# A convolution in two partial sums, one of them in PSUM, and new costs in the planner that orders the issue

## The chip, the core and the metric

The kernel runs on one core of a Trainium2 chip (trn2). The metric is the device time of one execution in microseconds; for the kernel before, three runs took 2491.57, 2493.82 and 2495.34 us, with a median of 2493.82.

## What is computed

One layer of a hybrid decoder, on 2048 prompt tokens with 16 meta tokens ahead of them and on 8 single tokens of running sequences. All data is float32.

```python
z = einsum('btd,dc->btc', rmsnorm(h, norm1_g), w_in)
q_r, f_r, i_r, g_r, a_r, b_r = split(z, IN_SPLITS)
o, s_new = hgrn2(q, k, v, logf, s0)                  # 4 heads of 128 x 128, in chunks of 64 tokens
y_hg = rmsnorm(o, hg_onorm_g) * silu(g_r)
glu = a_r * sigmoid(b_r)
xcat = concatenate([buf, glu], axis=1)
dw = depthwise_conv(xcat, conv_w) + conv_b           # 31 taps, 512 channels
y_cv = silu(layernorm(dw, conv_ln_g, conv_ln_b))
h = h + concatenate([y_hg, y_cv], axis=-1) @ w_out
h = h + square(relu(rmsnorm(h, norm2_g) @ w_up)) @ w_down
y = rmsnorm(h, final_g)
```

## The kernel before

**Phases.** The prompt is worked in four quarters of 512 tokens (`NQ`, `QT`). The mixing phase runs, for each quarter, 24 column pieces of `w_in` and 8 of `w_out`, in the order in(0), in(1), out(0), in(2), out(1), in(3), out(2), out(3). Each product of float32 is made of three passes with high and low parts, so a piece is 24 matmuls of 512 columns (in quarter 0, 48 of 260 or 268); these are the foreground matmuls. The MLP phase follows, in two halves of the tokens, with foreground matmuls nearly alone.

**Planner.** Nothing is left to a scheduler: the text emits every instruction in the order in which its engine takes it, and the order comes from an estimate that runs along in Python. `Model` keeps a time for each engine; `Proxy` gives each instruction a cost by its form and calls `Model.op`. Everything that isn't a foreground matmul is a generator in `Background`: it yields the name of the engine that it wants next, and `Background.ready` resumes it when the estimate says that its input is there and that the engine isn't too far ahead of TensorE. So the estimate never changes what is computed, only the place of each instruction in its engine's order. Where the foreground needs something that isn't done by the estimate, `Background.until` lets the estimate run on and emits background work, with no foreground matmul between, until it is.

**Heads.** `hgrn` is the chain of one head in one quarter: scan and reciprocal on VectorE (the tiles `B` and `I`), transposes of `I` on TensorE, score and state matmuls, then the head's output in a PSUM bank. That is normalised by four ScalarE squares with a sum (`junk,stat<-ps`), twelve VectorE instructions on 4 columns that make an inverse root (`rsqrt`, tiles `stat` and `kept`), four ScalarE scalings into `on`, which shares its buffer with `KPn`, and four TensorE transposes of it (`ps<-ident,KPn`). A head's tiles `F`, `K`, `Q`, `V` come from rings of two, so the head after next waits for it. The last product of a head is `ps<-Sch,Q`.

**Convolution.** `conv` works one quarter and one of four groups of 128 channels. Each of its 31 taps yields "any": if ScalarE and GpSimd have room by the estimate, ScalarE scales the shifted input by the tap's weight into a scratch buffer and GpSimd adds it (a side tap); otherwise VectorE does the tap in one instruction. All add into the same accumulator `acc_` in SBUF, one after the other:

```python
elif bg.choice == "dve" or len(scr.items) <= 3:
    V.scalar_tensor_tensor(out=acc_, in0=src, scalar=w, in1=acc_, op0=ALU.mult, op1=ALU.add)
else:
    t = scr.take()[0]
    S.activation(t, src, AF.Copy, scale=w)
    G.tensor_tensor(acc_, acc_, t, ALU.add)
```

`ln` normalises the four groups of a quarter when all are done; `out` of the quarter waits for it and for the heads. Background work has four PSUM banks. Scratch buffers of 512 columns: eleven, shared by accumulators, side taps and residuals.

In the views every instruction that the planner records has one line, L146 before and L167 after, so groups are told apart by their tiles: `scr<-glu,cw` is a tap.

Of the kernel before, what the change touches and what calls it, by code (L numbers as in the profile page):

```python
# [8 lines left out]
F32R = mybir.dt.float32r  # L9
# [68 lines left out]
class Model:  # L78
# [4 lines left out]
    def __init__(self):  # L83
        self.t = {"pe": 0.0, "dve": 0.0, "act": 0.0, "pool": 0.0, "dma": 0.0}
        self.cur = Ctx()
# [21 lines left out]
class Proxy:  # L107
# [3 lines left out]
    def __getattr__(self, f):  # L111
        fn, name, model = getattr(self._eng, f), self._name, self._model

        def call(*args, **kw):
# [6 lines left out]
            else:  # L121
                n = _size(out)
                if name == "pe":
                    rhs = kw.get("rhs")
                    if f == "transpose" or rhs.dtype != F32R:
                        cost = max(17 + 0.72 * n, 60.0) if f == "transpose" else max(1.67 * n, 214.0)
                        if n == 1:
                            cost = 425.0
                    else:
                        cost = 2.6 + 0.4167 * n  # L130
                elif name == "act":
                    cost = 130 + 0.8 * n
                    if not isinstance(kw.get("scale", 1.0), float):
                        cost += 100
                elif name == "pool":
                    cost = 60 + 2.2 * n
                elif f == "reciprocal":
                    cost = 60 + 6.3 * n
                elif f in ("bn_stats", "tensor_reduce"):
                    cost = 65 + 1.05 * _size(args[1])  # L140
                elif f in ("tensor_copy", "memset"):
                    cost = 65 + 0.53 * n
                else:
                    cost = 68 + 1.1 * n
                model.op(name, cost)
# [5 lines left out]
class Background:  # L151
# [13 lines left out]
    def ready(self, entry):  # L165
# [58 lines left out]
def tile_hybrid_step(  # L224
# [565 lines left out]
    with tc.manual_schedule():  # L790
# [3 lines left out]
        with ExitStack() as p1:  # L794
# [285 lines left out]
            dw = {}  # L1080
# [599 lines left out]
```

## Time and profile before

| | us |
|---|---|
| runs, median of 3 | 2493.82 |
| profiled execution, own time | 2496.16 |
| its span, first to last instruction | 2494.4 |
| PE busy, of the span | 2359.6 (95%) |
| DVE, ACT, POOL busy | 1192.5, 775.4, 750.4 |
| granted clock, mean share | 0.979 |

PE is TensorE, PEld its weight loads, DVE VectorE, ACT ScalarE, POOL GpSimd, SP SyncE, which issues the DMAs. A form is out<-in by the program's names, buffer numbers left out, with partitions x elements. The idle time in front of an instruction is given with what ended it. Busy time counts an instruction from start to end, so a VectorE instruction that is held up while it runs shows as a longer one, not as idle time.

### The profile page before, as it was taken

The numbers are of one execution on the slowest core, as the hardware profiler recorded it, in microseconds if no ns is written. First come the engines' busy times: TensorE is split into PE (matmuls) and PEld (weight loads), VectorE is DVE, ScalarE is ACT, GpSimd is POOL, SyncE is SP. The second block draws the span as 40 slices with busy tenths as digits, with TensorE's granted clock in tenths as the row PEclk, the third lists the DMA queues.
The fourth block names the chain that finished last, engine by engine and source line by source line (L and its number), as shares of the span: only waits on it lengthen the run. The fifth ranks groups of instructions, "written<-read, shape, count | busy, mean of one in ns | idle before, by whom it ended". The sixth has DMA issues, their size and how long they took to land.

```text
span 2494.4 us, 31897 instructions
## 1 busy us (share of the span) xinstructions
PE 2359.6 (95%) x13000; PEld 2101.0 (84%) x13000; DVE 1192.5 (48%) x1843; ACT 775.4 (31%) x1391; POOL 750.4 (30%) x476
## 2 busy tenths in 40 slices
PE   8877889899999699999999999999999999999998
PEld 8876777877777488999999999999888888888887
DVE  6798787657566964343233233225722122212225
ACT  6544566466546434312112112113201101100112
POOL 4565567667855721321222121221000000000000
PEclk9998999999999899999999999999999999999999
DMA  8664453853474257854444444447722222222222
GB/s 293 217 193 163 158 178 121 274 213 135 156 249 170 90 192 283 275 163 140 129 152 135 141 139 144 127 152 261 262 102 92 94 102 85 101 98 88 101 85 102
DMA packets 159224, 396.29 MB, mean 159 GB/s; under 512 B 8772, under 2 KB 107657, under 8 KB 125278
## 3 DMA queue, kind: packets, MB, share of 16 engines
q1 hardware_dynamic: 158934, 394.00, 46.4%
q8 instruction: 102, 1.67, 0.3%
q14 instruction: 44, 0.36, 0.0%
q10 hardware_dynamic: 144, 0.26, 0.0%
HBM read 265.91 MB, written 128.79 MB: 158 GB/s over the span
## 4 chain that ended last, share of the span: by engine, by line
PE 72%; DVE 17%; ACT 4%; DMA 3%; issue 2%; POOL 1%; SPq 0%; ACTq 0%; DVEq 0%; POOLq 0%
PE ps L146 72%; DVE scr L146 5%; DVE stat L146 3%; DVE kept L146 2%; ACT scr L146 2%; DVE I L146 1%; DMA raw<-in_w_in_dram 1%; DVE B L146 1%; DVE K L146 1%; DVE act L146 1%; DMA scr<-xscr 1%; POOL scr L146 1%; ACT act L146 1%; DVE glu L146 1%; DVE xn L146 1%
## 5 line engine op out<-in xcount | busy, mean ns | idle before, releaser
L146 PE MATMUL ps<-act,wsp 128*128 128x512 f32 (+5 forms) x7704 | 1504.7, 354 | 14.4 <-POOL wsp L146 8.1
L146 PEld LDWEIGHTS ps<-act,wsp 128*128 128x128 f32 x7704 | 1284.4, 191 | 176.6 <-POOL wsp L146 8.9
L146 PE MATMUL ps<-hid,wsp 128*128 128x344 f32 (+4 forms) x3864 | 713.4, 346 | 2.0 <-DMA wsp<-kw 1.9
L146 PEld LDWEIGHTS ps<-hid,wsp 128*128 128x128 f32 x3864 | 646.5, 188 | 64.8 <-DVE acc L146 1.5
L146 POOL TENSOR_TENSOR scr<-scr 128x512 f32<-128x512 f32 x330 | 466.6, 1434 | 265.2 <-ACT scr L146 202.3
L146 POOL TENSOR_TENSOR wsp<-raw,wsp 128x1024 fp32r<-128x1024 f32 (+1 forms) x98 | 237.5, 2424 | 589.6 <-ACT wsp L146 563.6
L146 DVE TENSOR_TENSOR acc<-ps,acc 128x1032 f32<-128x1032 f32 (+5 forms) x160 | 162.0, 1013 | 469.1 <-PE ps L146 469.0
L146 ACT ACTIVATE xn<-ps 128x1032 f32<-128x1032 f32 (+5 forms) x74 | 69.1, 934 | 838.1 <-PE ps L146 835.3
L146 DVE TENSOR_TENSOR xn<-xn 128x1032 f32<-128x1032 f32 (+3 forms) x68 | 80.3, 1181 | 508.0 <-ACT hid L146 508.0
L146 ACT ACTIVATE scr<-glu,cw 128x512 f32<-128x512 f32 x330 | 222.8, 716 | 19.2 <-POOL scr L146 15.8
L146 ACT ACTIVATE wsp<-raw 128x1024 fp32r<-128x1024 f32 (+1 forms) x98 | 101.5, 1036 | 302.9 <-PE ps L146 223.2
L146 DVE SCALAR_TENSOR_TENSOR scr<-glu,cw,scr 128x512 f32<-128x512 f32 x150 | 155.8, 1071 | 12.3 <-POOL scr L146 11.5
L146 DVE TENSOR_TENSOR hid<-xn,hid 128x1032 fp32r<-128x1032 f32 (+3 forms) x68 | 133.5, 1963 | 2.4
L146 ACT ACTIVATE junk<-ps 128x128 bf16<-128x128 f32 (+3 forms) x100 | 38.3, 383 | 109.7 <-PE ps L146 80.2
L146 ACT ACTIVATE hid<-xn 128x1032 fp32r<-128x1032 f32 (+3 forms) x68 | 69.0, 1015 | 2.2
L146 DVE TENSOR_TENSOR act<-scr,act 128x512 fp32r<-128x512 f32 (+1 forms) x36 | 33.2, 922 | 62.8 <-ACT act L146 62.8
L146 POOL TENSOR_TENSOR fg<-fg 128x512 f32<-128x512 f32 x28 | 36.8, 1315 | 58.7 <-ACT fg L146 58.7
L146 DVE RECIPROCAL I<-B 128x512 f32<-128x512 f32 (+1 forms) x16 | 54.0, 3378 | 0.6
L146 DVE TENSOR_TENSOR scr<-ps,scr 128x512 f32<-128x512 f32 x32 | 21.9, 685 | 62.3 <-DMA scr<-xscr 54.5
L146 PE MATMUL ps<-ident,I 128*128 128x128 f32 x64 | 10.9, 298 | 39.7 <-DVE I L146 39.7
L146 DVE TENSOR_SCALAR stat<-stat 128x4 int32<-128x4 int32 (+5 forms) x94 | 27.7, 297 | 36.9 <-ACT junk L146 35.3
L146 PEld LDWEIGHTS ps<-ident,I 128*128 128x128 f32 x64 | 7.8, 150 | 43.4 <-DVE I L146 37.4
(190 smaller groups left out, 1326.9 us busy)
## 6 DMA issues: line engine op xcount, KB each, us to landing
wsp<-kw SPq DMA_DIRECT2D x167, 1024.0 KB
kw<-wsp SPq DMA_DIRECT2D x96, 1024.0 KB
raw<-in_w_up_dram SPq DMA_DIRECT2D x32, 512.0 KB
raw<-in_w_down_dram SPq DMA_DIRECT2D x32, 512.0 KB
raw<-in_w_in_dram SPq DMA_DIRECT2D x24, 512.0 KB
out_dram<-xn SPq DMA_DIRECT2D x18, 512.0 KB
scr<-xscr SPq DMA_DIRECT2D x32, 256.0 KB
hscr<-scr SPq DMA_DIRECT2D x32, 256.0 KB
```

Source lines behind the costliest of these rows:

```text
L146: return fn(*args, **kw)
```

## The change

It has two parts. The convolution of a group becomes two generators that take taps from the two ends of one list: one sums in a PSUM bank on VectorE, the other in the scratch accumulator by ScalarE and GpSimd; one VectorE instruction merges them. A gate lets one group at a time in. And the costs in `Proxy` get other numbers, with a `port` in `Model.op` that the estimate gives to one instruction at a time, GpSimd's or a VectorE one that lies in SBUF alone.

```diff
-    def op(self, e, cost):
+    def op(self, e, cost, port=False):
         c = self.cur
         start = max(self.t[e], c.t + (self.SEM if c.e not in (None, e) else 0.0))
+        if port:
+            start = max(start, self.port)
+            self.port = start + cost
...
-                        cost = 2.6 + 0.4167 * n
+                        cost = max(3 + 0.4455 * n, 108.0)
...
-                    cost = 60 + 2.2 * n
+                    cost, port = 190 + 2.17 * n, True
...
-                else:
-                    cost = 68 + 1.1 * n
+                    port = all(x.space == bass.MemoryType.SB for x in tiles)
...
+                    elif f == "scalar_tensor_tensor" and not isinstance(kw["scalar"], float):
+                        cost = 205 + 1.05 * n
...
-        if e == "any":
-            self.choice = "pool"
-            if r <= now and max(t["act"], t["pool"]) < now + self.SPARE:
-                return True
-            self.choice = "dve"
-            return r <= max(t["dve"], now) and t["dve"] < now + self.HORIZON
+        if e == "side":
+            return r <= now and max(t["act"], t["pool"]) < now + self.SPARE
...
             def conv(q, c):
                 yield from until(("const",))
+                yield from take1(cgate)
                 while len(scr.items) <= 3:
                     yield "poll"
+                acc_ = dw[q, c] = scr.take()[0]
+                b = (yield from take(banks))[0]
+                taps, left_ = list(range(TAPS)), [2]
+                bg.add(conv_part(q, c, taps, left_, True, acc_, b), 4 + q)
+                bg.add(conv_part(q, c, taps, left_, False, acc_, b), 4 + q)
...
+                    j = taps.pop(0 if vector else -1)
+                    if vector and n == 0:
+                        V.tensor_scalar(ps[:, b, :], src, w, cb[:, c:c + 1], ALU.mult, ALU.add)
+                    elif vector:
+                        V.scalar_tensor_tensor(out=ps[:, b, :], in0=src, scalar=w, in1=ps[:, b, :],
+                                               op0=ALU.mult, op1=ALU.add)
...
+                yield from until(("part", q, c, not vector))
+                yield "dve"
+                V.tensor_tensor(acc_, ps[:, b, :], acc_, ALU.add)
+                banks.give(b)
+                cgate.give(0)
```

Numbers of instructions, over the whole program: VectorE taps 156 before, 208 after, with 16 merging sums (the form `scr<-ps,scr`, 32 before, 48 after); ScalarE's tap scalings 340 before, 288 after; GpSimd's tap adds 330 before, 272 after. Of VectorE's subtractions into `act` 19 move to GpSimd. All other forms keep their numbers.

**The order on TensorE**, at head 1 of quarter 2, before, from the last pair of the head's output products to after the transposes of its normalised rows:

```order
L146 MATMUL ps<-vn,scT 128x128
L146 MATMUL ps<-Sch,Q_118 128x128
L146 MATMUL ps<-act,wsp_88 128x512 x21
L146 MATMUL ps<-act,wsp_86 128x512 x6
L146 MATMUL ps<-ident,KPn 128x128 x4
L146 MATMUL ps<-act,wsp_86 128x512 x18
```

The same place of the changed program:

```order
L167 MATMUL ps<-vn,scT 128x128
L167 MATMUL ps<-Sch,Q_118 128x128
L167 MATMUL ps<-ident,KPn 128x128 x4
L167 MATMUL ps<-act,wsp_88 128x512 x21
L167 MATMUL ps<-act,wsp_86 128x512 x12
```

The 27 foreground matmuls (`act,wsp`) that stood between the head's products and its transposes now follow the transposes.

**The order on ScalarE**, same head, before, around the squares (`junk,stat`) and the scaled rows (`KPn<-ps,kept`); `scr<-glu,cw` are side taps:

```order
L146 ACTIVATE Sch<-Sst 128x128
L146 ACTIVATE scr<-glu,cw 128x512
L146 ACTIVATE a_t<-ps 128x512
L146 ACTIVATE scr<-glu,cw 128x512 x2
L146 ACTIVATE junk,stat<-ps 128x128 x4
L146 ACTIVATE scr<-glu,cw 128x512 x2
L146 ACTIVATE KPn<-ps,kept 128x128 x4
```

And in the changed program:

```order
L167 ACTIVATE scr<-glu,cw 128x512 x4
L167 ACTIVATE Sch<-Sst 128x128
L167 ACTIVATE scr<-glu,cw 128x512 x2
L167 ACTIVATE junk,stat<-ps 128x128 x4
L167 ACTIVATE scr<-glu,cw 128x512 x13
L167 ACTIVATE KPn<-ps,kept 128x128 x4
```

Between the squares and the scaled rows stood two side taps; now thirteen.

**The order on VectorE**, same head, in the changed program, in the middle of the twelve steps (`stat`, `kept`):

```order
L167 TENSOR_SCALAR kept<-stat 128x4
L167 SCALAR_TENSOR_TENSOR ps<-glu,cw,ps 128x512
L167 SCALAR_TENSOR_TENSOR stat<-stat,kept 128x4
L167 SCALAR_TENSOR_TENSOR ps<-glu,cw,ps 128x512
L167 TENSOR_TENSOR stat<-stat,kept 128x4
```

A tap of the sum in PSUM stands between any two steps of the head's inverse root.

## Rows read from the trace of the kernel before

**Rows 1.** The page: busy tenths of TensorE (PE) in 40 slices of 62 us.

```profile
PE   8877889899999699999999999999999999999998
```

**Rows 2.** Stretches: length, busy us of PE, PEld, DVE, ACT, POOL, clock, DMA.

```profile
0.00:1020.00 1020.00, 899.61 (x5024) 773.17 (x5025) 717.63 (x1221) 533.98 (x1088) 593.28 (x411) 0.95 0.57 194
1020.00:2495.00 1475.00, 1460.02 (x7978) 1327.79 (x7976) 474.88 (x623) 241.45 (x304) 157.09 (x65) 1.00 0.40 134
...
140.00:230.00 90.00, 60.79 (x416) 58.26 (x416) 86.68 (x121) 38.07 (x86) 46.97 (x28) 0.83 0.52 163
...
820.00:860.00 40.00, 16.23 (x83) 13.55 (x82) 39.53 (x40) 13.70 (x22) 30.77 (x20) 0.70 0.17 60
```

**Rows 3.** What TensorE waits for from 0 to 1020 us: total, times, longest.

```profile
PE ps L146 <- DVE I L146: 39.7, 8, 23.8
PE ps L146 <- ACT KPn L146: 22.7, 9, 10.4
```

**Rows 4.** Timeline of TensorE at 818 to 850 us: start, us, what [idle before].

```profile
818.17 7.20 PE L146 MATMUL ps<-act,wsp 128*128 128x512 f32 x30
849.14 1.11 PE L146 MATMUL ps<-ident,I 128*128 128x128 f32 x4 [23.77 <-DVE I L146]
849.90 2.72 PE L146 MATMUL ps<-act,wsp 128*128 128x512 f32 x6
```

**Rows 5.** Timeline of VectorE (DVE) at 796 to 866 us.

```profile
796.71 34.83 DVE L146 SCALAR_TENSOR_TENSOR scr<-glu,cw,scr 128x512 f32<-128x512 f32 x29
...
864.07 1.21 DVE L146 SCALAR_TENSOR_TENSOR stat<-stat,kept 128x4 f32<-128x4 f32 x1
865.32 0.16 DVE L146 TENSOR_TENSOR stat<-stat,kept 128x4 f32<-128x4 f32 x1
865.52 0.16 DVE L146 SCALAR_TENSOR_TENSOR kept<-stat,kept 128x4 f32<-128x4 f32 x1
```

**Rows 6.** By tile, the taps' weights (cw): count, min/median/max ns.

```profile
L146 ACT ACTIVATE scr<-glu,cw x330: 703/713/762, 39.6 to 897.1; 128x512 f32<-128x512 f32 x165
L146 DVE SCALAR_TENSOR_TENSOR scr<-glu,cw,scr x150: 653/746/2907, 49.1 to 884.4; 128x512 f32<-128x512 f32 x150
```

**Rows 7.** By tile, small steps (kept): count, min/median/max ns.

```profile
L146 DVE TENSOR_TENSOR stat<-stat,kept x144: 140/161/1279, 26.8 to 2488.3; 128x4 f32<-128x4 f32 x48, 128x2 f32<-128x2 f32 x45, 128x1 f32<-128x1 f32 x42, 8x1 f32<-8x1 f32 x6
```

**Rows 8.** By tile, vectors (vec): one input in PSUM.

```profile
L146 DVE SCALAR_TENSOR_TENSOR Sg<-ps,vec,Sg x16: 733/750/753, 149.2 to 966.7; 128x512 f32<-128x512 f32 x16
```

**Rows 9.** Forms of VectorE, 0 to 1020 us: busy us, mean ns | idle before.

```profile
L146 DVE SCALAR_TENSOR_TENSOR scr<-glu,cw,scr 128x512 f32<-128x512 f32 x150 | 155.8, 1071 | 12.3 <-POOL scr L146 11.5 <-ACT scr L146 0.2
...
L146 DVE TENSOR_TENSOR scr<-ps,scr 128x512 f32<-128x512 f32 x32 | 21.9, 685 | 62.3 <-DMA scr<-xscr 54.5 <-PE ps L146 7.8
```

**Rows 10.** Forms of GpSimd (POOL), 0 to 1020 us.

```profile
L146 POOL TENSOR_TENSOR scr<-scr 128x512 f32<-128x512 f32 x330 | 466.6, 1434 | 265.2 <-ACT scr L146 202.3 <-DVE scr L146 31.9 <-DVE kept L146 10.3
```

**Rows 11.** Timeline of TensorE at 621 to 629 us, one head's cover.

```profile
621.35 6.49 PE L146 MATMUL ps<-act,wsp 128*128 128x512 f32 x27
628.75 1.10 PE L146 MATMUL ps<-ident,KPn 128*128 128x128 f32 x4 [0.91 <-ACT KPn L146]
```

**Rows 12.** Timeline of VectorE, first and last step of that head.

```profile
623.23 2.04 DVE L146 TENSOR_SCALAR stat<-stat 128x4 f32<-128x4 f32 x2 [3.66 <-ACT junk L146]
...
628.13 0.16 DVE L146 SCALAR_TENSOR_TENSOR kept<-stat,kept 128x4 f32<-128x4 f32 x1
```

**Rows 13.** Timeline of VectorE at 205 to 210 us, steps between taps.

```profile
205.27 1.24 DVE L146 TENSOR_SCALAR stat<-stat 128x4 int32<-128x4 int32 x1
...
210.07 0.15 DVE L146 SCALAR_TENSOR_TENSOR stat<-stat,kept 128x4 f32<-128x4 f32 x1
```

**Rows 14.** Timeline of TensorE at 216 us.

```profile
215.90 1.25 PE L146 MATMUL ps<-ident,KPn 128*128 128x128 f32 x4 [10.38 <-ACT KPn L146]
```

**Rows 15.** Timeline of GpSimd at 801 us.

```profile
801.00 1.68 POOL L146 TENSOR_TENSOR scr<-scr 128x512 f32<-128x512 f32 x1 [0.70 <-DVE scr L146]
803.37 1.67 POOL L146 TENSOR_TENSOR scr<-scr 128x512 f32<-128x512 f32 x1 [0.69 <-DVE scr L146]
```

More of the change, by code (lines that the diff above doesn't have):

```diff
@@ L122, in call @@
                 n = _size(out)
+                port = False
                 if name == "pe":
                     rhs = kw.get("rhs")
[L125 to L128, printed above, removed]
+                    if f == "transpose":
+                        cost = 109.0
+                    elif rhs.dtype != F32R:
+                        cost = max(1.75 * n, 222.0)
@@ L145, in call @@
-                model.op(name, cost)
+                    ap = kw.get("in_", args[1] if len(args) > 1 else None)
+                    cost = 185 + 0.8333 * n
+                    if ap is not None and ap.space == bass.MemoryType.PSUM:
+                        cost -= 15
+                    for x in ("scale", "bias"):
+                        if not isinstance(kw.get(x, 1.0), (float, int)):
+                            cost += 93
+                    if "accum_out" in kw:
+                        cost += 194
+                elif name == "pool":
+                    cost, port = 190 + 2.17 * n, True
+                else:
+                    tiles = [x for x in list(args) + [kw.get(k) for k in ("out", "in0", "in1")]
+                             if hasattr(x, "space") and x.space is not None]
+                    n = max(_size(x) for x in tiles)
+                    port = all(x.space == bass.MemoryType.SB for x in tiles)
+                    if f == "reciprocal":
+                        cost, port = 75 + 6.4 * n, False
+                    elif f == "tensor_tensor_scan":
+                        cost = 60 + 4.0 * n
+                    elif f in ("bn_stats", "tensor_reduce"):
+                        cost, port = 150 + 1.05 * n, False
+                    elif f in ("tensor_copy", "memset", "tensor_scalar"):
+                        cost = 150 + (0.55 if port else 1.05) * n
+                    elif f == "scalar_tensor_tensor" and not isinstance(kw["scalar"], float):
+                        cost = 205 + 1.05 * n
+                    else:
+                        cost = 155 + 1.045 * n
@@ L146, in call @@
+                model.op(name, cost, port)
             return fn(*args, **kw)
@@ new lines, in conv_part @@
+            def conv_part(q, c, taps, left_, vector, acc_, b):
+                base = META if q == 0 else 0
+                n = 0
+                while True:
+                    yield "dve" if vector else "side"
+                    if not taps:
+                        break
+                    if not vector and n and len(scr.items) <= 3:
+                        yield "poll"
+                        continue
+                    j = taps.pop(0 if vector else -1)
+                    src, w = glu[:, c, base + j:base + j + QT], cw[:, c, j:j + 1]
+                    if vector and n == 0:
[3 more added lines that the diff above has]
+                                               op0=ALU.mult, op1=ALU.add)
+                    elif n == 0:
+                        S.activation(acc_, src, AF.Copy, scale=w)
@@ L1098, in conv @@
                     else:
                         t = scr.take()[0]
+                        model.cur.t = 0.0
                         S.activation(t, src, AF.Copy, scale=w)
@@ L1102, in conv @@
                         scr.give(t)
+                        model.cur.t -= 1300.0
+                    n += 1
+                if not vector and n == 0:
+                    S.memzero(acc_)
+                done.add(("part", q, c, vector))
+                left_[0] -= 1
+                if left_[0]:
+                    return
+                yield from until(("part", q, c, not vector))
[3 more added lines that the diff above has]
+                cgate.give(0)
                 if q < NQ - 1:
```

21 lines of the change are left out of this document (2 added, 19 removed).

## The prediction

> **What bounds the kernel now.** I read the page first, then the stretches, then TensorE's waits, then the timelines around the longest of them. The slices [rows 1] show TensorE between 6 and 8 tenths busy up to about 560 us, near full to 800 us, a dip to 6 tenths once more, and full afterwards. The stretches [rows 2] put numbers on it: of the 1020 us of the mixing phase TensorE is busy 899.6, so 120.4 us are idle; of the remaining 1475 us only 15 are. Whatever the change can give or take lies in those 120.4 us, because the matmuls are the same. Two stretches are dense with idle time: 140 to 230 us (29.2 us idle, VectorE busy 86.7 of 90) and 820 to 860 us (23.8 us idle, VectorE 39.5 of 40). There VectorE is the bound.
>
> What TensorE waits for [rows 3] is led by VectorE's inverse decay I (39.7 us, one wait of 23.8) and by ScalarE's normed rows KPn (22.7 us). Both belong to the chain of one head. The longest wait [rows 4]: 30 matmuls, then nothing until the four transposes of I start at 849.14. VectorE in that time [rows 5] works through taps: 29 in 34.83 us, 1.20 us each, and the chain stands behind them in its order. In the same rows a step on 4 columns takes 1.21 us at 864.07 and 0.16 at 865.32. What differs is GpSimd. By tile [rows 6 to 8], the taps that lie wholly in SBUF take between 653 and 2907 ns, the small steps between 140 and 1279, but a form with one operand in PSUM (Sg, 16 times) between 733 and 753. So a VectorE instruction on SBUF alone waits for a running GpSimd add, and one that touches PSUM doesn't.
>
> **The change, part by part.**
>
> *The taps.* Before, 156 taps on VectorE and 340 on ScalarE, of which 330 are added by GpSimd; now 208 and 288, of which 272 are added, and 16 merging sums. VectorE: 150 taps at 1.071 us [rows 9] become 192 that I price by the Sg row, whose operation and operands are the nearest, at 0.75 (below that 0.685, the row of the form that the merging sums have; above, 1.071, should they still wait for GpSimd). With the first taps, some 161 us become 192 x 0.75 + 16 x 0.75 + 16 x 0.685 = 167. ScalarE loses 52 x 0.71 = 37 us, GpSimd 58 x 1.434 = 83 [rows 6, 10]. All of this lies beside TensorE, which has 12,639 instructions in both programs, as SyncE has 559. None of it is a gain by itself; what counts is where TensorE's own order puts an instruction that waits for it.
>
> *The order.* TensorE takes its instructions in the order written. After a head's last recurrence matmuls come, for that head: four sums of squares on ScalarE, twelve small VectorE steps (the inverse root, all in SBUF), four scalings on ScalarE (KPn), and four transposes on TensorE. The chain is covered by as many foreground matmuls as stand between. Before, every head has 18 to 108 between, 24 to 36 in eleven of the sixteen. One such head shows what the cover does [rows 11]: the 27 matmuls take 6.49 us, the transposes start at 628.75, and the wait is 0.91. From 621.35 to 628.75 the chain took 7.4 us; VectorE's twelve steps had 5.0 of it, from 623.23 to 628.29 [rows 12], and the squares and scalings around them 2.4.
>
> Now the matmuls between are, for the four heads of the quarters in turn: 150, 0, 54, 0; 81, 18, 270, 66; 93, 0, 120, 156; 9, 0, 45, 0. Five heads have no cover at all, two have a short one. And the chain is longer: in ScalarE's order 13 side taps stand between the squares and KPn of head 1 of quarter 0, 16 and some 21 in the next two heads, 11 in head 1 of quarter 1, 13 in head 1 of quarter 2, 12 in head 0 of quarter 3, where before it was mostly 2 to 4. VectorE's twelve steps have a tap of the PSUM sum between any two.
>
> *The price of an uncovered chain.* Around the steps 2.4 us. The steps start 0.2 us apart with GpSimd idle and take 1.21 to 1.24 each when an add holds them [rows 5, 13]. In these places 11 to 21 adds run back to back, and the tap between two steps (0.75) leaves time for the next add to start, so I take all steps as held: 12 x 1.24 + 2.4 = 17.3. From below, the nearest row is the chain of head 1 of quarter 0 before, with nine taps between its steps and few adds: TensorE waited 10.4 us for it [rows 14]. From above, tap and held step one behind the other, 12 x (1.24 + 0.75) + 2.4 = 26. I take 18, since GpSimd's own queue gives nearly the same: 13 adds at 1.434 are 18.6.
>
> The Trainium skill, page "SBUF — State Buffer", section "SBUF: two separate sides", has a rule that speaks against this change: VectorE and GpSimd take turns on a shared pair of ports, for a whole instruction each, and the loser is blocked entirely. By it a step would wait out every full add. Two SBUF taps and an add would then need 2 x 0.746 + 1.434 = 2.9 us, while the adds of the stretch at 800 us start 2.37 us apart [rows 15]: the trace disagrees on the "entirely". By the rule each step would cost 1.43, and the six places some 14 us more in all, 2545.
>
> *The places, wait by wait* (cover at 6.49 / 27 = 0.24 us per matmul [rows 11]):
> - quarter 0, head 1, and quarter 2, head 1: no cover, 18 each.
> - quarter 3, head 0: 9 matmuls, 2 us of cover, 16.
> - quarter 1, head 1: 11 adds, 15.8, less 18 matmuls (4.3), 12.
> - quarter 0, head 2: 16 adds, 22.9, less 54 matmuls (13.0), 10.
> - quarter 0, head 3: ScalarE's KPn stands behind 21 side taps, each waiting for a scratch buffer that an add frees: 21 x 1.434 = 30.1, less four buffers in flight (5.7), about 24.
> - quarter 0, head 0: seven steps, some 30 transposes and VectorE's tile work stand in one place, with only four GpSimd subtractions: between 5 and 18, I take 12.
> - quarter 3, heads 1 and 3: no taps are left beside them, the bare chain, 5 each.
>
> Together 120 us.
>
> *What goes.* The waits for I and KPn in their old places, 62.4 us, are replaced by this list: taps of 0.75 instead of 1.20 take the 23.8 at 849 us away, and the dense stretch at 140 us is loosened, though it is the same taps, now emitted later, that fill the places of quarter 0. The other 58.0 us of waits (scratch, weights, start-up) come from handshakes of 1 to 3 us; fewer steps are written ahead of their data now, so I keep two thirds, 38 (30 to 58).
>
> **Sum.** Idle 120 + 38 = 158 us against 120.4, so the mixing phase grows by 37.6 and the rest stays: its 1475 us have 15 idle. The profiled execution took 2496.2 us, its span 2494.4; with 37.6 it is 2533.8. The runs' median lies 2.3 us below the profiled one, so I forecast 2531 us. After a long wait the granted clock is at 0.70 [rows 2], between the levels of 1.2 and 2.4 GHz, and the first six matmuls take 2.72 us instead of 1.44 [rows 4]: some 3 us per long wait. Before, the dips at 140 to 230 us (0.83) cost the same kind of time; I set both equal and leave 0 to 20 us more to the range.
>
> **The rivals.**
> 1. *The steps slip through.* If GpSimd doesn't run back to back, because ScalarE feeds it late, a step costs 0.2 and a place is the old exposed chain of 10.4 at most: 10.4 twice, 8.3, 6.2, 0, 24, 5, 5 and 5 make 74; with 30 of other waits 104, 16 us less than before: 2478. For it speaks that among the steps at 205 to 210 us one is held and another takes 0.15 [rows 13]. Against it: there nine SBUF taps kept GpSimd off, and these taps no longer do. It decides at a mean step of about 0.6 us: the 37.6 us spread over some 60 steps are 0.6 each, and below 1.24 - 0.6 the change gains. Chance 0.15.
> 2. *The waits only move.* Quarter 0 loses as much in the dense stretch as its places cost, and the lost 23.8 at 849 us pays for quarters 1 to 3: within 0.2% of 2494. About 0.2% is what a measurement of this kernel can tell from no change. Chance 0.07.
> 3. *Longer still.* The clock after eight long waits instead of two costs 20 us more: 2551. Chance 0.13.
> 4. *It doesn't do what it says*: a tap with its sum in PSUM still waits for GpSimd, since it reads its data and weight from SBUF. Then 208 taps cost 1.07 and the places some 25 us more: 2556. The Sg row with its spread of 20 ns speaks against it. Chance 0.03.
>
> **How the numbers follow.** The forecast has 0.62; its own range is 2505 to 2550, from places between 95 and 140 us. Slower by over 0.2%: 0.62 + 0.13 + 0.03 = 0.78; the same 0.07; faster 0.15. The range reaches from 2490, which leaves out most of rival 1, to 2560.
>
> **What would show it.** Right: TensorE's waits for KPn grow from 22.7 us to over 80 and lead the list; the wait at 849 us for I is gone; PSUM taps stand at 0.75 with a narrow spread; the small steps' mean rises over 0.6 us. Wrong: KPn waits of 10 us and less, small steps at 0.3 on the mean, or idle time of the mixing phase below 120 us.

## The result and the profile after

The changed kernel takes 2512.64 us (median of 4 runs, 2509.37 to 2514.38) against 2493.16 us for the kernel before in the same session: ratio 1.0076, interval 1.0059 to 1.0093. It is slower by 19.5 us where the forecast said slower by 37; the time lies in the range, on the forecast's side.

The stretches of the kernel after, cut at 1040 us because its mixing phase ends some 15 us later than before (columns as in [rows 2]):

```profile
0.00:1040.00 1040.00, 904.24 (x5056) 783.35 (x5057) 684.92 (x1274) 510.73 (x1042) 515.20 (x374) 0.92 0.56 192
1040.00:2513.00 1473.00, 1455.97 (x7946) 1323.97 (x7944) 470.06 (x619) 235.15 (x297) 155.37 (x64) 1.00 0.40 134
```

TensorE idles for 1040 - 904.2 = 135.8 us of the mixing phase, 15.4 more than before [rows 2], and for 17.0 us afterwards, 2 more. Its busy time over the whole span is 2360.2 us, before 899.61 + 1460.02 = 2359.6: the matmuls cost the same, so the loss is idle time. VectorE, ScalarE and GpSimd are all less busy than before (VectorE 1155.0 us in the sum of these two lines), and the kernel is slower all the same.

What TensorE waits for, from 0 to 1040 us (total, times, longest), answering to [rows 3]:

```profile
PE ps L167 <- ACT KPn L167: 84.3, 10, 18.9
PE ps L167 <- ACT scr L167: 24.3, 4, 13.9
PE ps L167 <- POOL fg L167: 6.6, 1, 6.6
...
PE ps L167 <- DVE I L167: 2.9, 1, 2.9
```

The list is turned round: the inverse decay I fell from 39.7 to 2.9 us, the normed rows KPn rose from 22.7 to 84.3. Four of these waits, in TensorE's timeline (start, us, what, [idle before <- releaser]):

```profile
206.36 0.99 PE L167 MATMUL ps<-ident,KPn 128*128 128x128 f32 x3 [18.87 <-ACT KPn L167]
...
319.55 1.12 PE L167 MATMUL ps<-ident,scr 128*128 128x128 f32 x4 [13.91 <-ACT scr L167]
...
666.16 1.25 PE L167 MATMUL ps<-ident,KPn 128*128 128x128 f32 x4 [18.80 <-ACT KPn L167]
...
896.74 1.25 PE L167 MATMUL ps<-ident,KPn 128*128 128x128 f32 x4 [4.44 <-ACT KPn L167]
```

The first and third are the uncovered heads 1 of quarters 0 and 2, with taps beside them; the second is head 3 of quarter 0, where other tiles queue behind side taps; the last is head 1 of quarter 3, uncovered as well, but with all taps done: 4.44 us is the bare chain. What fills the other 14 us is in VectorE's timeline of the first of them:

```profile
190.90 0.24 DVE L167 TENSOR_SCALAR stat<-stat 128x4 f32<-128x4 f32 x1
191.06 0.74 DVE L167 SCALAR_TENSOR_TENSOR ps<-glu,cw,ps 128x512 f32<-128x512 f32 x1
191.71 0.77 DVE L167 TENSOR_SCALAR stat<-stat 128x4 int32<-128x4 int32 x1
192.40 0.74 DVE L167 SCALAR_TENSOR_TENSOR ps<-glu,cw,ps 128x512 f32<-128x512 f32 x1
193.06 0.78 DVE L167 TENSOR_SCALAR kept<-stat 128x4 int32<-128x4 int32 x1
...
205.15 0.76 DVE L167 SCALAR_TENSOR_TENSOR kept<-stat,kept 128x4 f32<-128x4 f32 x1
```

and in GpSimd's:

```profile
189.85 17.38 POOL L167 TENSOR_TENSOR scr<-scr 128x512 f32<-128x512 f32 x13 [2.78 <-ACT scr L167]
```

A small step and a tap of the PSUM sum alternate. Before, such a step took 0.16 us or, held, 1.21 [rows 5]; here each takes 0.77. From 191.06 to 205.15 VectorE's pairs start 1.34 us apart, and GpSimd's 13 adds take 17.38 / 13 = 1.337 each. **One step goes through per add.** The tap isn't held (0.74 us each time), but it fills the moment between two adds in which the next step could have gone; e4 and e5 below take the two apart.

ScalarE had made its 13 side taps by 197.26 and then stood idle for the last step:

```profile
205.94 1.14 ACT L167 ACTIVATE KPn<-ps,kept 128x128 f32<-128x128 f32 x4 [8.69 <-DVE kept L167]
```

So the steps on VectorE ended this wait, not the side taps in ScalarE's order; it is the same at head 1 of quarters 1 and 2 and at head 0 of quarter 3 (5.23, 7.34 and 8.76 us of idle ScalarE). At heads 2 and 3 of quarter 0 it is the other way round: there ScalarE reaches KPn only after side taps that wait for a scratch buffer from GpSimd.

The forms of VectorE and GpSimd from 0 to 1040 us (count | busy us, mean ns), answering to [rows 9, 10]:

```profile
L167 DVE SCALAR_TENSOR_TENSOR ps<-glu,cw,ps 128x512 f32<-128x512 f32 x192 | 143.6, 748 | 3.1
...
L167 DVE SCALAR_TENSOR_TENSOR stat<-stat,kept 128x4 f32<-128x4 f32 x48 | 25.8, 538 | 0.4
```

```profile
L167 POOL TENSOR_TENSOR scr<-scr 128x512 f32<-128x512 f32 x272 | 363.4, 1336 | 213.5 <-ACT scr L167 191.4 <-issue 7.7
```

The taps in PSUM stand at 748 ns where those in SBUF stood at 1071.

### The profile page after: what moved, and what is told of

It reads as the page before. It is cut to its first block, busy times and chain, and to the rows that moved or that the text cites. A ratio compares the mean times of both kernels' runs of the same rounds, so it can differ in the third digit from the quotient of the medians.

```text
span 2512.5 us, 31830 instructions
## 1 busy us (share of the span) xinstructions
PE 2360.2 (94%) x13000; PEld 2107.3 (84%) x13000; DVE 1155.0 (46%) x1892; ACT 745.9 (30%) x1339; POOL 670.6 (27%) x437
## 4 chain that ended last, share of the span: by engine, by line
PE 73%; DVE 4%; DMA 1%; ACT 1%; issue 0%; POOL 0%; POOLq 0%; ACTq 0%; DVEq 0%
PE ps L167 73%; DVE ps L167 1%; DVE stat L167 1%; DMA wsp<-kw 1%; DVE kept L167 0%; POOL scr L167 0%; DVE xn L167 0%; DVE act L167 0%; ACT scr L167 0%; DVE I L167 0%; DMA hscr<-scr 0%; ACT junk L167 0%; DVE scr L167 0%; DVE B L167 0%; DVE K L167 0%
## 5 line engine op out<-in xcount | busy, mean ns | idle before, releaser
L167 POOL TENSOR_TENSOR scr<-scr 128x512 f32<-128x512 f32 x272 | 363.4, 1336 | 213.5 <-ACT scr L167 191.4
L167 ACT ACTIVATE scr<-glu,cw 128x512 f32<-128x512 f32 x288 | 191.0, 714 | 7.7 <-POOL scr L167 5.8
L167 DVE SCALAR_TENSOR_TENSOR ps<-glu,cw,ps 128x512 f32<-128x512 f32 x192 | 143.6, 748 | 3.1
L167 PE MATMUL ps<-ident,KPn 128*128 128x128 f32 (+1 forms) x66 | 16.8, 378 | 84.3 <-ACT KPn L167 84.3
L167 PEld LDWEIGHTS ps<-ident,KPn 128*128 128x128 f32 (+1 forms) x66 | 10.3, 163 | 91.1 <-ACT KPn L167 87.5
L167 DVE TENSOR_TENSOR scr<-ps,scr 128x512 f32<-128x512 f32 x48 | 33.0, 687 | 108.2 <-DMA scr<-xscr 71.0
L167 DVE SCALAR_TENSOR_TENSOR stat<-stat,kept 128x2 f32<-128x2 f32 (+4 forms) x144 | 49.8, 349 | 1.9
L167 DVE SCALAR_TENSOR_TENSOR kept<-stat,kept 128x2 f32<-128x2 f32 (+4 forms) x153 | 46.4, 306 | 2.1
```

The lines of the kernel that those rows point to most:

```text
L167: return fn(*args, **kw)
```

## The experiments

The question was where the loss comes from. **Theory A**: from the order. The planner's new durations with their port leave heads without cover, and in such a place the chain goes at the pace of GpSimd's adds. **Theory B**: from the two sums themselves (taps between the steps, one group at a time, a bank that is held). **Theory C**, for one run: the VectorE taps between the steps make the chain long, whatever GpSimd does. All runs were timed beside the kernel before, whose medians were 2496.9, 2497.2 and 2498.3 us in the three sessions, so ratios are compared, not times.

### The two halves of the change, each alone

**e1** is the changed kernel with the convolution of the kernel before (all taps into one tile of SBUF, each to whichever engine is free):

```diff
-                bg.add(conv_part(q, c, taps, left_, True, acc_, b), 4 + q)
-                bg.add(conv_part(q, c, taps, left_, False, acc_, b), 4 + q)
...
+                for j in range(TAPS):
+                    yield "any"
...
```

> The new durations and the shared port alone; the convolution stays one sum of SBUF tiles. Theory A (the durations and the port order the work so that heads are left without cover; there, a step of the chain goes through once per GpSimd add): in the program's order five heads now have no foreground matmul between their last recurrence product and their transposes, with 26, 20, 25, 25 and 25 side taps beside them, and ScalarE's KPn stands behind those. At 1.34 us an add that is 36, 31, 35, 34 and 35 us, with some 25 in shorter places: about 200 us of idle time in places against 115 in the changed kernel, so 2590 us (2560 to 2610). Theory B (the two sums do it: taps between the steps, one quarter block at a time, a bank that is held): without them the time is that of before or below, 2480 to 2496.

Measured: 2618.71 us, ratio 1.0488 (1.0473 to 1.0504). Waits for KPn in the first 1040 us, and GpSimd's and VectorE's timelines beside the longest of them, at head 0 of quarter 3:

```profile
PE ps L167 <- ACT KPn L167: 143.8, 10, 36.4
```

```profile
923.52 44.34 POOL L167 TENSOR_TENSOR scr<-scr 128x512 f32<-128x512 f32 x31
```

```profile
936.93 1.22 DVE L167 TENSOR_SCALAR stat<-stat 128x4 int32<-128x4 int32 x1
938.07 1.83 DVE L167 SCALAR_TENSOR_TENSOR scr<-glu,cw,scr 128x512 f32<-128x512 f32 x1
939.83 1.23 DVE L167 TENSOR_SCALAR kept<-stat 128x4 int32<-128x4 int32 x1
```

31 adds stand in one run, 1.43 us each, and TensorE waits 36.4 us through it. The time is 29 us above theory A's figure and 9 above its range. The places are theory A's, the prices aren't: at this head a step and the SBUF tap behind it are both held, 2.90 us together, so one step goes through per two adds. The five long places cost 28.5, 14.4, 17.3, 26.0 and 36.4 us, 122.6 in all, where 171 were priced, and waits for other tiles (scr 19.7, dg 15.9, F 8.8, I 8.0) more than make up for it. So e1 shows that this planner loses without the two sums; it doesn't show the pace of one step per add.

**e2** is the changed kernel with the durations of the kernel before and no port:

```diff
-                    cost, port = 190 + 2.17 * n, True
+                    cost = 60 + 2.2 * n
...
-                    elif f == "scalar_tensor_tensor" and not isinstance(kw["scalar"], float):
-                        cost = 205 + 1.05 * n
...
+                else:
+                    cost = 68 + 1.1 * n
```

> The two sums alone; the planner keeps its old durations and knows no port. Theory A: in the program's order every head has at least 27 matmuls of cover, 27 to 120, with 0 to 6 side taps, so at 6.5 us of cover or more and 6 adds at most a chain of 8 to 14 us is nearly hidden: waits for KPn below 15 us in all, idle time of the mixing phase 60 to 95 us, 2435 to 2470 us, faster than both kernels. Theory B: the taps of 0.75 us that stand 10 to 15 at a time between the steps of five heads cost as in the changed kernel: 2505 to 2520, with KPn waits over 50 us.

Measured: 2452.82 us, ratio 0.9821 (0.9803 to 0.984). The first 1040 us, and the waits in them (the line that records every instruction is L151 in this kernel and L168 in e6; e7's half adds stand at L1137):

```profile
0.00:1040.00 1040.00, 956.32 (x5418) 834.76 (x5419) 733.02 (x1417) 464.64 (x970) 380.23 (x269) 0.96 0.60 205
```

```profile
PE ps L151 <- ACT KPn L151: 18.9, 5, 10.6
...
PE ps L151 <- DVE dg L151: 17.0, 6, 7.0
```

Idle time is 83.7 us, within its range; KPn has 18.9 us where under 15 were expected. The half of the change that puts the sum in PSUM is worth 1.8%, and the half with the measured durations costs 4.9% alone and 2.6% on top of it. Theory B is out: the sums by themselves lose nothing.

### What of the planner's half does it

**e9** is the changed kernel with the port taken out of `Model.op`:

```diff
-        if port:
+        if False:
             start = max(start, self.port)
```

> The changed kernel with its measured durations and its two sums, but the planner knows no port (nothing else is changed). In the program's order only quarter 0 heads 1 and 3 and quarter 3 head 3 have no cover now, the others 15 to 216 matmuls. If the port in the planner is what takes the cover away: places of 15 us (quarter 0 head 1, 9 adds), 8 (head 3), 4 (quarter 3 head 3), 10 (quarter 0 head 0) and some 10 in short ones, others 20 to 30: idle time of the mixing phase 70 to 80 us, 2452 us (2438 to 2475). If the durations alone do it: 2500 to 2515.

Measured: 2474.66 us, ratio 0.9903 (0.9886 to 0.9921), the upper edge of the first expectation, though idle time is 101.5 us where 70 to 80 were expected; waits for KPn 36.1 us, 18.5 of it at head 1 of quarter 0. Of the 2.6% the port in the estimate costs 1.7% and the durations the rest. The estimate with a port holds up each chain behind every add that it has issued, takes the head for late, lets TensorE run out of other matmuls, and issues the next taps meanwhile, which makes the head later still. That last loop is read from the planner's code (side taps stay ready while the foreground waits); that it is the reason was not tried by itself.

### Holding the taps while a head is in its chain

**e3** is the changed kernel with a counter of the heads that stand between their squares and their KPn, and no tap written while it isn't zero; **e4** holds only the side taps (`norming[0] and not vector`), **e5** only VectorE's (`norming[0] and vector`; it also lets a side tap wait for a free scratch buffer before it asks for the side engines, not after):

```diff
+                norming[0] += 1
                 yield "act"
                 ss = sc(4)
...
+                norming[0] -= 1
                 banks.give(bo)
...
+                    while taps and norming[0]:
+                        yield "poll"
                     yield "dve" if vector else "side"
                     if not taps:
                         break
+                    if norming[0]:
+                        continue
```

> The changed kernel, but no new tap of either sum is written while a head stands between its squares and its KPn. The same heads stay without cover. Theory A: with no adds and at most 5 VectorE taps beside it, the uncovered chain is the bare one, 4.4 to 7 us: five such places 28 us, quarter 0 head 0 10 us, others 20 to 30: idle time of the mixing phase 60 to 70 us against 135.8, so 2445 us (2430 to 2465), VectorE's steps at 0.16 to 0.25 us there. Theory B: the work that is held comes later all at once and the gate of one block passes it on: 2500 to 2515.

Measured: 2444.53 us, ratio 0.979 (0.9773 to 0.9806). Head 1 of quarter 0 in VectorE's and TensorE's timelines:

```profile
193.93 0.17 DVE L167 TENSOR_SCALAR kept<-stat 128x4 int32<-128x4 int32 x1
194.13 0.16 DVE L167 SCALAR_TENSOR_TENSOR stat<-stat,kept 128x4 f32<-128x4 f32 x1
194.33 0.17 DVE L167 TENSOR_TENSOR stat<-stat,kept 128x4 f32<-128x4 f32 x1
```

```profile
196.34 1.25 PE L167 MATMUL ps<-ident,KPn 128*128 128x128 f32 x4 [4.46 <-ACT KPn L167]
```

No add runs, the steps start 0.2 us apart, and the wait of 18.87 us is 4.46. Idle time in the first 1040 us falls from 135.8 to 74.7 us. Five heads still stand without cover, though not quite the same ones: head 1 of quarter 2 has 39 matmuls now, head 1 of quarter 1 none. What stood between the steps is gone, and with it more than the loss; the hold also moves the held taps elsewhere, and how much of the gain comes from that was not told apart.

> The changed kernel, but only the side taps (ScalarE's products with GpSimd's adds) are held while a head stands in its chain; VectorE's PSUM taps go on between the steps. If the pace of an uncovered chain is GpSimd's add together with the tap that fills the time between two adds, then without adds a step takes 0.16 us and a step with its tap 0.9: 12 x 0.9 + 2.4 = 13 us in quarter 0 head 1, 13 in quarter 1 head 1, 10 in quarter 3 head 0, 1 in quarter 2 head 1 (48 matmuls now), 7 in quarter 0 head 3, 3 in quarter 3 head 1, 10 in quarter 0 head 0: 57 us, with 20 others 77, so 2455 us (2440 to 2475), slower than with both held (2444.5). If the taps alone set the pace: the places keep 17 to 19 us, 2490 to 2515.

Measured: 2459.45 us, ratio 0.9851 (0.9836 to 0.9866). VectorE's timeline at head 1 of quarter 0:

```profile
191.32 0.16 DVE L167 TENSOR_SCALAR stat<-stat 128x4 int32<-128x4 int32 x1
191.45 0.76 DVE L167 SCALAR_TENSOR_TENSOR ps<-glu,cw,ps 128x512 f32<-128x512 f32 x1
192.11 0.17 DVE L167 TENSOR_SCALAR kept<-stat 128x4 int32<-128x4 int32 x1
```

Without adds a step and its tap take 0.79 us a pair, and the wait there is 15.3 us rather than the 13 expected: ahead of the chain VectorE stands 3 us behind the merging sum, which waits for the last add.

> The changed kernel, but only VectorE's PSUM taps are held while a head stands in its chain; the side taps with their adds go on. Theory A (one step per add): the steps still go through one per add, 12 x 1.34 + 2.4 = 18.5 us with or without taps between them; places in quarter 0 head 1 18, head 3 33 (26 side taps), quarter 1 head 1 6, quarter 2 head 1 17, quarter 3 heads 0 and 1 12 and 13, quarter 0 head 0 10: 109 us, 2495 to 2525. Theory C (the VectorE taps between the steps make the chain long): 12 steps at 0.2 us, 5 to 8 us a place: 2455 to 2480.

Measured: 2526.03 us, ratio 1.0117 (1.0102 to 1.0132): 1 us above theory A's range, and far from C's. But the traces show each theory half right. At head 1 of quarter 3, VectorE:

```profile
896.23 0.16 DVE L167 SCALAR_TENSOR_TENSOR stat<-stat,kept 128x4 f32<-128x4 f32 x1
896.43 1.12 DVE L167 TENSOR_TENSOR stat<-stat,kept 128x4 f32<-128x4 f32 x1
897.58 0.16 DVE L167 SCALAR_TENSOR_TENSOR kept<-stat,kept 128x4 f32<-128x4 f32 x1
897.78 1.12 DVE L167 SCALAR_TENSOR_TENSOR stat<-stat,kept 128x4 f32<-128x4 f32 x1
...
906.96 0.69 DVE L167 TENSOR_TENSOR scr<-ps,scr 128x512 f32<-128x512 f32 x1 [6.52 <-POOL scr L167]
```

With no tap between, a step is held to the end of an add (1.12 us) and **the one behind it slips through as well** (0.16): two steps per add, 1.35 us for both, not one. The twelve steps at head 1 of quarter 0 took 5.3 us instead of 15.0, seven of them before the first add (GpSimd waited 3.18 us for ScalarE there), and 6.3 us at head 1 of quarter 2, beside adds; TensorE's waits at these two were 8.64 and 11.45 us instead of 18.87 and 18.80. That is theory C's half: without the taps the steps are quick. What the kernel gained there it lost elsewhere: fewer taps go to VectorE (147 instead of 208), ScalarE and GpSimd have 61 more. A merging sum that waits 6.52 us for them gets between the steps (last line), and at head 3 of quarter 0 the steps are done at 318.60 but ScalarE reaches KPn at 332.59, behind side taps; TensorE waits 24.7 us for it, the longest wait of this run. So the add and the tap are both needed for the slow pace of the steps: e3 takes away both, e4 the add, e5 the tap.

### The sum in SBUF, in the same order; and shorter adds

In **e6** and **e7** every engine keeps the order of the changed kernel. e6 changes where VectorE's sum lies:

```diff
-                        V.scalar_tensor_tensor(out=ps[:, b, :], in0=src, scalar=w, in1=ps[:, b, :],
+                        V.scalar_tensor_tensor(out=vsum, in0=src, scalar=w, in1=vsum,
                                                op0=ALU.mult, op1=ALU.add)
```

> Every engine's instructions in exactly the order of the changed kernel, but VectorE's sum lies in a tile of SBUF instead of PSUM (to make room for it, the tile that takes the unused squares is of bytes, and the ring of small statistics has 96 columns instead of 104). If a PSUM operand is what frees the tap from GpSimd: the 192 taps take 1.0 to 1.3 us on the mean instead of 0.748, with a maximum over 2 us; VectorE has some 85 us more; in an uncovered chain a step and a tap go through per add, and the add waits for the tap, about 2.1 us a step, 28 us instead of 18.8 in quarter 0 head 1 and quarter 2 head 1: 2560 us (2535 to 2590). If the place of the sum doesn't matter and only the order does: taps at 0.75 and 2505 to 2520.

Measured: 2561.94 us, ratio 1.026 (1.0243 to 1.0277). The form of the tap from 0 to 1040 us, and the same place in VectorE's and GpSimd's timelines:

```profile
L168 DVE SCALAR_TENSOR_TENSOR vsum<-glu,cw,vsum 128x512 f32<-128x512 f32 x192 | 199.9, 1041 | 3.1
```

```profile
203.87 0.74 DVE L168 SCALAR_TENSOR_TENSOR vsum<-glu,cw,vsum 128x512 f32<-128x512 f32 x1
204.54 1.22 DVE L168 TENSOR_SCALAR kept<-stat 128x4 int32<-128x4 int32 x1
205.67 0.74 DVE L168 SCALAR_TENSOR_TENSOR vsum<-glu,cw,vsum 128x512 f32<-128x512 f32 x1
```

```profile
198.77 23.17 POOL L168 TENSOR_TENSOR scr<-scr 128x512 f32<-128x512 f32 x13 [2.94 <-ACT scr L168]
```

In one order the place of the sum is worth 1.8% (1.026 / 1.0076), some 46 us: 748 ns against 1041 for a tap. It works both ways: the 13 adds that took 17.38 us now take 23.17, because each lets a tap by; a step and a tap take 1.80 us, and the wait is 26.0 us. (In e1 it was the tap that waited, 1.83 us, beside adds of 1.43: which of the two gives way isn't fixed.)

e7 changes the size of GpSimd's instruction:

```diff
-                        G.tensor_tensor(acc_, acc_, t, ALU.add)
+                        for o in (0, QT // 2):
+                            s_ = slice(o, o + QT // 2)
+                            nc.gpsimd.tensor_tensor(acc_[:, s_], acc_[:, s_], t[:, s_], ALU.add)
```

> Every other engine's instructions in exactly the order of the changed kernel; each of GpSimd's 272 adds of the convolution is split in two over half the columns, one right after the other, so the same sums are made with more GpSimd time. If a step waits for the end of one GpSimd instruction and the tap behind it (0.74) lets the next one begin, a chain goes at one step per half add, about 0.9 us a step instead of 1.37: 13 us in quarter 0 head 1 and quarter 2 head 1, 11 in quarter 3 head 0, some 8 in quarter 1 head 1, so 20 us less, and 3 to 8 us more where ScalarE waits for scratch (quarter 0 heads 2 and 3): 2497 us (2485 to 2510). If VectorE is held by the amount of GpSimd's work, whatever its pieces: the places keep 18 us or grow, 2512 to 2535.

Measured: 2507.97 us, ratio 1.0037 (1.0022 to 1.0052), against 1.0076 (1.0059 to 1.0093) for the changed kernel. VectorE and GpSimd at head 1 of quarter 0:

```profile
189.68 0.70 DVE L167 TENSOR_SCALAR kept<-stat 128x4 int32<-128x4 int32 x1
190.29 0.74 DVE L167 SCALAR_TENSOR_TENSOR ps<-glu,cw,ps 128x512 f32<-128x512 f32 x1
190.95 0.15 DVE L167 SCALAR_TENSOR_TENSOR stat<-stat,kept 128x4 f32<-128x4 f32 x1
191.07 0.76 DVE L167 SCALAR_TENSOR_TENSOR ps<-glu,cw,ps 128x512 f32<-128x512 f32 x1
```

```profile
185.52 20.61 POOL L1137 TENSOR_TENSOR scr<-scr 128x256 f32<-128x256 f32 x30 [1.73 <-ACT scr L167]
```

Held and free steps now alternate: two steps and two taps in 2.05 us, as long as three half adds (20.61 / 30 = 0.687 each). The twelve steps take 11.7 us instead of 15.0, although GpSimd's adds cost 402.6 us in all instead of 363.4: here the pace hangs on the ends of GpSimd's instructions, not on the amount of its work. It is no rule, though. At two other places of this run a VectorE instruction got in at none of these ends:

```profile
264.08 8.79 DVE L167 SCALAR_TENSOR_TENSOR kept<-stat,kept 128x2 f32<-128x2 f32 x1
...
320.78 13.51 DVE L167 TENSOR_TENSOR act<-scr,act 128x512 fp32r<-128x512 f32 x1 [10.85 <-ACT act L167]
```

```profile
305.08 28.66 POOL L1137 TENSOR_TENSOR scr<-scr 128x256 f32<-128x256 f32 x42 [2.28 <-ACT scr L167]
```

A step of 0.15 us and a product of 0.69 us were held through 13 and 20 half adds, until the run of adds was over (at 272.85 and 333.74). No other run holds VectorE for so long. The half adds follow each other without a gap (0.72 us each, 0.69 apart), the whole ones of the changed kernel leave 0.08 us (1.26 each, 1.34 apart); whether that is the reason no run shows.

The time is another matter too. The waits at head 1 of quarters 0, 1 and 2 and head 0 of quarter 3 are 16.6, 7.2, 15.1 and 16.5 us, where I expected 13, 8, 13 and 11; that is 9.2 us less than in the changed kernel. But KPn of head 3 of quarter 0, whose last steps stand behind the product that was held for 13.51 us, now waits 12.1 us instead of 2.8, and KPn is at 84.2 us in all, as it was. Idle time is the same; the 6.3 us by which the span is shorter are TensorE's busy time (2354.1 instead of 2360.2 us), and why that is I can't say. So the run shows the pace at these heads, what it can cost elsewhere, and no gain that comes from it.

### Other combinations

Four more kernels complete the table of sums, durations and hold. **e8** is e2 and **e10** is e9, both held as in e3. **e12** is the kernel before and **e13** is e1, both held at the one place where their convolution takes a tap:

```diff
+                    while True:
+                        while norming[0]:
+                            yield "poll"
-                    yield "any"
+                        yield "any"
+                        if not norming[0]:
+                            break
```

> The two sums with the planner's old durations and no port, and no tap written while a head stands in its chain. One head (quarter 0 head 3) has no cover now, the others 24 to 90 matmuls, with 0 to 5 VectorE taps: KPn waits under 10 us against 18.9 with the sums alone; nothing else is aimed at, so 2442 us (2430 to 2455). If holding gives nothing where the cover is there already: 2448 to 2458.

Measured: 2446.42 us, ratio 0.9788 (0.9766 to 0.981), inside the range; whether the hold adds anything to the two sums alone (0.9803 to 0.984) these intervals don't settle. KPn fell from 18.9 to 1.4 us as expected, but the waits for scratch rose from 18.7 to 36.2.

> As the one without the port, and no tap of either sum is written while a head stands in its chain. Every head but quarter 3 head 3 now has 15 matmuls or more, 0 to 5 VectorE taps and 0 to 3 side taps: waits for KPn below 10 us in all, idle time of the mixing phase 45 to 60 us: 2430 us (2415 to 2445), the fastest so far. If holding only moves the work to places where it delays other tiles (scr, dg, I): 2445 to 2465.

Measured: 2446.35 us, ratio 0.9799 (0.9782 to 0.9815), not the fastest. A miss: 1 us above the first range, just inside the second. KPn still has 15.3 us, idle time is 69.8 us instead of 45 to 60, and small waits for dg, I, kept and QS (10.7, 7.4, 7.3, 5.2) take the rest.

> The kernel before (one sum in SBUF, old durations, no port), with no tap written while a head stands in its chain. Its waits for KPn are 22.7 us and fall to about 8; its waits for I (39.7 us), which the dense stretches of SBUF taps cause, stay; VectorE has 208 SBUF taps in place of 156: 2485 us (2470 to 2500). If holding is what gives the gain of the held kernels and the sum in PSUM adds nothing: 2440 to 2455.

Measured: 2484.77 us, ratio 0.9947 (0.9929 to 0.9964), as expected: the waits for I stay at 40.4 us. Holding alone is worth 0.5% with one sum and the old durations; the rest of what e8 gains comes with the two sums. Whether the bank, the two lists or the gate does it was tried for the bank only, and only in the changed order (e6).

> The new durations and the port with one sum in SBUF, which took 2618.7 us, and no tap written while a head stands in its chain. Six heads are still without cover, with 6 taps or fewer beside them: bare chains of 4.5 to 6 us, 30 us instead of 143.8 us of waits for KPn: 2505 us (2485 to 2530). If the loss sits in the taps' places elsewhere: 2560 or more.

Measured: 2614.36 us, ratio 1.0458 (1.0429 to 1.0487): over 100 us above the first figure, so the second case. The waits, and VectorE's timeline in the longest, 39.51 us of TensorE up to 453.11:

```profile
PE ps L167 <- ACT scr L167: 65.6, 13, 39.5
PE ps L167 <- DVE I L167: 40.0, 4, 35.3
PE ps L167 <- ACT glu L167: 34.7, 2, 33.2
PE ps L167 <- ACT KPn L167: 24.7, 11, 5.9
```

```profile
411.82 13.90 DVE L167 SCALAR_TENSOR_TENSOR scr<-glu,cw,scr 128x512 f32<-128x512 f32 x21
...
425.72 18.63 DVE L167 SCALAR_TENSOR_TENSOR scr<-glu,cw,scr 128x512 f32<-128x512 f32 x28
```

KPn did fall from 143.8 to 24.7 us. But with one sum and the port in the estimate the convolution itself falls behind, and VectorE makes up 49 taps in a row while TensorE, ScalarE and GpSimd stand: the loss moved. The hold repairs a plan whose convolution fits beside the chains; under these durations it does with two sums (e3) and doesn't with one.

The versions e3, e8 and e10 are about 2% faster than the kernel before, and their intervals overlap. The two sums alone already give 1.8%.

## Why the prediction was right, and half of it too large

**The places** held: forecast 120 us, measured 112.3. In the prediction's list, forecast and measured (from TensorE's timeline): quarter 0 head 1 18 and 18.87, quarter 2 head 1 18 and 18.80, quarter 3 head 0 16 and 16.02, quarter 1 head 1 12 and 10.96, quarter 0 head 2 10 and 5.08, quarter 0 head 3 24 and 23.68 (five waits, the longest the 13.91 above), quarter 0 head 0 12 and 9.99 (four waits), quarter 3 heads 1 and 3 5 and 4.44 each. The cover that the order shows was the right thing to read. Two entries owe something to luck: the 12 of quarter 0 head 0 was a guess between 5 and 18, and at quarter 0 head 3 KPn itself waits 2.76 us; 18.16 us of the rest are for two scr tiles in ScalarE's order behind the same side taps.

**The term that failed** is "the other 58.0 us of waits", of which "I keep two thirds, 38 (30 to 58)". Measured: 135.8 - 112.3 = 23.5 us, below its lower end. Before, dg, wsp, xn, F, Sch and QS had 11.8, 8.1, 6.5, 2.9, 2.4 and 2.3 us of waits there, 34.0 together; after, 1.8 for xn and 0.4 for Sch are what is left of them. I took a third of such waits away, because fewer steps are written ahead of their data; three fifths went. Why isn't settled. That the other engines catch up while TensorE stands in a long wait would do it (in e3, with the same durations and the long waits gone, dg is back at 8.1 us), but e1 has long waits and 15.9 us of dg all the same. The largest wait outside the places is now fg with 6.6. In sums: places 7.7 less, other waits 14.5 less, 22.2 of the 37.6 us; the rest of the program idled 2.0 us more, and busy time is 0.6 more. So the profiled execution took 2514.2 us instead of 2533.8. The runs' median lies 1.6 us below it, where 2.3 was set.

**The price of a chain** came out right (18.87 for 18) by a working that was only half right. The prediction had 12 held steps of 1.24 one behind the other, with the taps costing nothing beside them, and "GpSimd's own queue" as the second figure, 13 adds. GpSimd's pace is right, 1.34 us, but what counts is the steps, one per add; that 12 steps and 13 adds are nearly the same number is luck, since ScalarE was done with its side taps 8.69 us before the last step. The held step itself shows as 0.77, since the tap ahead of it has already used up the rest of the add. So the sign "the small steps' mean rises over 0.6 us" failed: the 128x4 steps stand at 0.39 to 0.54.

**The Trainium skill's rule** (page "SBUF — State Buffer", section "SBUF: two separate sides"): where VectorE's instruction has two inputs in SBUF or runs in a two-port mode, the loser of the shared ports waits out a whole instruction. I set it aside because of the 2.37 us between adds [rows 15]. In the places it came closer than I thought: a step waits for the end of one add each time, 1.34 us a step where the rule gave 1.43, and in e1 a step and an SBUF tap wait out an add each. What it leaves out is e5's second step per add.

**The other signs**: KPn leads with 84.3 us (over 80 was set), the wait for I at 849 us is gone, PSUM taps have a mean of 748 ns (0.75). Rival 1 (steps slip through) decided itself by the places: steps show shorter than 1.24 us, but a place with taps and adds is as long as forecast. Rival 2 (waits only move): no; 0.76% is outside its 0.2%, but part of it is so: handshakes paid for part of the places. Rival 3 (clock): the granted clock of the phase is 0.92 instead of 0.95, but TensorE's busy time is the same within 0.6 us. The prediction's "some 3 us per long wait" was too much: the six matmuls of [rows 4] cost 1.28 us more, and the next six, at 853.26, take 1.65 us again. Rival 4 (PSUM taps wait): no; e6 shows what it would have cost. Two counts of the prediction differ from the traces, and nothing rests on them: both kernels show 13,000 matmuls on TensorE, the same number but not 12,639, and the 161 us of VectorE's taps leave out six first taps of the kernel before.

**What the prediction didn't ask** is which half of the change makes the places. It named the order and took both halves together; e1, e2 and e9 show that the planner's half loses more than the sums gain.

## What to carry to other kernels

Before costing a scheduler's change by the work it moves, count what stands in the issue order between a chain's producer and its consumer; the places without cover, at the pace of the slowest neighbour in them, gave the main term here within 7%. A better estimate of durations (a tap on VectorE is now put at 743 ns, before at 631, and in PSUM it takes 748) can make a greedy planner worse, if it fills the time in which it waits with work that makes what it waits for later; holding such work while a short critical chain is open took the ratio from 1.0076 to 0.979 here. And the small waits are no fixed share to carry over: beside the new long ones they fell from 58.0 to 23.5 us, which was most of my error.

## What the runs showed of the hardware

- VectorE and GpSimd, both on SBUF: in e5 a held step takes 1.12 us of which 0.16 is its own work, so an add that starts every 1.34 us shuts VectorE out for some 0.96 us and leaves, as an estimate from these numbers, about 0.4, room for two steps of 0.2. With a full SBUF tap in the gap either can be the one that waits: the add in e6 (1.78 us per add, the tap at 0.74), the tap in e1 (1.83, the adds at 1.43).
- On the whole the same matmuls cost TensorE more busy time in kernels that idle more: 2352.7 us with 90.3 us of idle time (e3), 2360.2 with 152.3 (the changed kernel), 2365.4 with 195.3 (e6), 2369.5 with 248.1 (e1), 2375.5 with 237.3 (e13), and the granted clock over the span is 0.978 in e3 and 0.945 in e1. Between 120 and 155 us of idle time it doesn't hold: e7 has 2354.1 with 152.1, e12 2363.5 with 122.6, the kernel before 2359.6 with 134.8.
- A tap with its data and weight in SBUF and its sum in PSUM isn't held at all: 672 to 760 ns over 192 taps, most of them beside adds. With the sum moved to PSUM a tap took 0.29 us less on the mean in the same order (1041 - 748).
- With adds of half the columns (0.687 us each, back to back) twelve steps took 11.7 us instead of 15.0, with 11% more GpSimd time; but in the same run (e7) two VectorE instructions of 0.15 and 0.69 us were held 8.79 and 13.51 us, to the end of the run of adds. Shorter instructions on GpSimd don't by themselves let VectorE in more often.
